# One transfer for each head: the bias table of a neighbourhood attention, stored as each query and head needs it

## The chip, the cores and the metric

The kernel runs on one core of one Trainium2 chip. The metric is the time of one execution on the device in microseconds (us); the median of three runs of the kernel before is 2916.8 us (2911.22 to 2920.01). The core has TensorE (PE, with its weight loads shown as PEld), VectorE (DVE), ScalarE (ACT), GpSimd (POOL) and SyncE (SP). SP computes nothing: it issues the transfers, and 16 DMA engines carry them out.

## The reference, cut to what matters

An encoder layer with two attention branches. The one that matters here is the neighbourhood attention: 8 heads of 64 channels over a grid 64 columns wide (2048 tokens of a sample and 512 of a prompt, so 32 and 8 rows). A query sees a window of 8 rows and 16 columns, and to each score a learned bias is added that depends on head, row distance and column distance alone:

```python
drow = key_rows - r[:, None]
dcol = jnp.clip(kc - qcol[:, :, None], -(NA_COLS - 1), NA_COLS - 1)
bias = rel_bias[h_idx, r_idx, c_idx].astype(jnp.float32)
s = jnp.einsum('brnqhd,brknchd->brnqhkc', qb, kb).astype(jnp.float32) / math.sqrt(dh) + bias
s = jnp.where(col_ok[:, :, None, None, :], s, NEG)
```

The other branch is a dilated band attention in three groups. Both are weighted by gates, projected, merged and projected again.

## The kernel before, in words

**Stages.** `run` goes through the dilated branch (`dil_sweeps`), the neighbourhood branch (`na_sweeps`), the gates and branch projections (`gate_sweeps`) and the last projection (`out_sweep`). `na_sweeps` works in two halves of four heads. In each half it goes over 20 tiles of 128 tokens (16 of the sample, 4 of the prompt): `bank` multiplies a tile by the q and k weights (512 columns) and by the v weights (256 columns), and `na_qk` and `na_v` normalise the result, split it into two fp16 parts and turn it by transposing transfers (`qn<-qs`, `kT<-qs`) or store it (`vd<-v`). Once six tiles are there, `na_group` starts the attention of 8 grid rows: 4 column blocks of 128 queries (8 rows by 16 columns), each in units of one head or two.

**Where the bias enters.** `load_bias` (L977) fills a table `G`, 128 queries by 4 heads by 16 by 48 values of float32. Partition `16 i + c` belongs to the query in row `i` and column `c` of a block, and holds a 16 by 48 cut of the padded, reversed bias of each head. ACT scales the four heads of `G` in place (`scale`, L991). `bias` in `na_group` (L1148) then lets POOL add a mask to a window of `G` and write `bm`, which DVE adds to the scores (`e<-s,bm`). There is one `G`; the second half's table goes to the same place, and its load is started when the 60 additions of the first half are planned (`na_bias`, L933).

In memory the table is `bias`, 8 row shifts by 8 heads by 16 by 63 values. `load` (L983) is called four times, `BIAS_STEP` = 4 us of planned time apart, and issues two transfers each time. Each fills 16 partitions with 64 pieces of 48 values (192 bytes), so a half takes 8 transfers with 1024 pieces each. The four scalings are planned after the fourth call, 4 us apart.

**What sets the order.** Each engine carries out its instructions in the order in which they were emitted, and nothing is put in another order at run time. That order comes from a planner (`Clock`, L109): every step is put on a heap with a due time, and each instruction adds a planned cost to its engine's time. A transfer (`dma`, L388) costs SP 0.48 us and the DMA engines its bytes at 340,000 a us (`D_RATE`), without regard to the size of its pieces, and counts as landed 1.2 us after that. Other steps hang on gates: the additions on `bias_ready` (L932, four signals, one from each scaling), a unit's scores on its additions (`go`, L1232).

**What runs beside it.** Right after the first half's table is called for, `na_weights(1)` (L961) loads the weights of the second half in two banks: each `load_bank` (L422) issues `wr<-in_w_in` transfers of 256 KB in pieces of 1 KB or 2 KB, DVE takes maxima of them (`wm`), PE turns the maxima (`across`, L474, a transpose at L356) and spreads them, and ACT and DVE make the fp16 weights `wt`. Beside the second half's table, `gate_weights(0)` does the same for the gates. All of these, the transposing transfers and the table are issued by SP, one after the other, on one queue.

Of the kernel before, what the change touches and what calls it, by code (L numbers as in the profile page):

```python
# [104 lines left out]
BIAS_STEP = 4.0  # L105
# [159 lines left out]
class Enc:  # L265
# [711 lines left out]
    def load_bias(self, half):  # L977


        G = self.G = self.N["g"].tile([128, 4, 16, 48], F32, name="G")  # L980
        t = self.a["bias"]

        def load(qr):  # L983
            for i in range(qr, qr + 2):
                self.dma(G[16 * i:16 * i + 16],
                         AP(t.tensor, (8 * i + 4 * half) * 16 * 63, [[1, 16], [63, 64], [1, 48]]))
            if qr == 6:
                for h in range(4):
                    self.clk.at(self.clk.done + BIAS_STEP * h, scale, h)

        def scale(h):  # L991
            self.act(G[:, h], G[:, h], scale=self.sc[0][:, 2:3])
            self.bias_ready[half].signal()

        for i in range(4):
            self.clk.at(self.clk.now + BIAS_STEP * i, load, 2 * i)

    def na_v(self, R, seq, i, ps):
        half = seq["half"]
# [1078 lines left out]
def masks():  # L2078
    m = np.zeros((128, C_W), np.float32)
    q = np.arange(128)[:, None]  # L2080
    j = np.arange(256)[None]
    band = np.where((j >= q) & (j <= q + 128), 0, NEG)
    m[:, C_BAND:C_BAND + 256] = band
    m[:, C_BAND + 256:C_BAND + 384] = band[:, 0:128]
    j = np.arange(128)[None]
    m[:, C_B1:C_B1 + 128] = np.where(np.abs(j - q) <= 64, 0, NEG)
    m[:, C_BD:C_BD + 128] = np.where(j // 32 == q // 32, 0, NEG)
    cols, _ = window_masks()
    m[:, C_COL:C_COL + 96] = np.concatenate(cols, axis=1)
    return m  # L2090
# [15 lines left out]
def na_masks():  # L2106
    cols, rows = window_masks()
    m = [np.minimum(r[:, k0:k0 + n, None], c[:, None]).reshape(128, -1)
         for r, k0, n in zip(rows, (4, 0, 0), ROWS) for c in cols]
    return np.concatenate(m, axis=1).astype(ml_dtypes.bfloat16)  # L2110
# [9 lines left out]
def rope_table():  # L2120
    inv = np.array(INV_BITS, np.uint32).view(np.float32)
    ang = (np.arange(LS, dtype=np.float32)[:, None] * inv[None]).astype(np.float64)
    c, s = np.cos(ang), np.sin(ang)
    return np.ascontiguousarray(np.concatenate([c, c, -s, s], axis=1).astype(np.float32))


def arrays_of(inputs):
    b = np.zeros((8, 23, 63), np.float32)
    b[:, 4:19, 16:47] = np.asarray(inputs["rel_bias_a"])[0][:, ::-1, ::-1]

    b = np.stack([b[:, r:r + 16] for r in range(8)])
    a = {
        "x_prompt": np.asarray(inputs["x_prompt"])[0],
        "x_sample": np.asarray(inputs["x_sample"])[0],
        "norm_gain": inputs["norm_gain"],
        "w_in": np.asarray(inputs["w_in"])[0],
        "qn_a": inputs["qn_a"],
        "kn_a": inputs["kn_a"],
        "qn_b": inputs["qn_b"],
        "kn_b": inputs["kn_b"],  # L2140
        "w_a": np.asarray(inputs["w_branch_a"])[0],
        "w_b": np.asarray(inputs["w_branch_b"])[0],
        "w_out": np.asarray(inputs["w_out"])[0],
        "bias": b,
        "ident": np.eye(128, dtype=np.float32),
        "cmask": masks(),
        "namask": na_masks(),
        "cs": rope_table(),
    }
    return {k: np.ascontiguousarray(v) for k, v in a.items()}  # L2150
# [24 lines left out]
```

## Time and profile before

| | |
|---|---|
| median of the runs | 2916.8 us |
| the profiled execution's own time | 2913.82 us |
| its span, first to last instruction | 2912.0 us |
| PE busy | 2687.4 us (92%) |
| DVE, ACT, POOL busy | 1627.4, 1303.5, 1269.4 us |
| mean granted TensorE clock | 0.975 |
| DMA | 823504 packets, 419.20 MB, mean 144 GB/s |
| packets under 512 B | 706240 |
| `G<-in_bias` | 16 transfers of 192 KB |

Times in the trace are counted from the first instruction of the span. A busy share over the whole span mixes stages: the dilated branch lasts to about 1285 us, the neighbourhood branch to about 1850 us, and the gates and the last projection fill the rest. A line of waits names the engine that stood, and behind the arrow what ended its wait. SP's own rows carry a q (SPq), and their duration is the time it took to issue a transfer, not the time in which the data moved.

### The profile page before, as it was taken

Reading aid. Unit: us, or ns where it says so; the run is one execution under the profiler, and the core shown is the slowest. Engines: PE = TensorE matmul, PEld = TensorE weight load, DVE = VectorE, ACT = ScalarE, POOL = GpSimd, SP = SyncE. Lnnn points to the kernel's source line nnn. Section 1 sums busy time; section 2 is a strip of 40 time slices with the busy share of each in tenths; the row PEclk is TensorE's granted clock in tenths of the full one; section 3 lists DMA queues with packets and bytes.
Section 4 is the critical chain, followed back from the end, with each engine's and each line's share of the span. In section 5 each row is a group of like instructions: output and inputs, shape, how many; then the busy total and the mean of one; then the engine's idle time right before and its main releaser. Section 6 shows DMA issues by size and latency. Waiting matters only on the chain.

```text
span 2912.0 us, 55755 instructions
## 1 busy us (share of the span) xinstructions
PE 2687.4 (92%) x20841; PEld 1785.7 (61%) x20841; DVE 1627.4 (56%) x3902; ACT 1303.5 (45%) x3495; POOL 1269.4 (44%) x1787
## 2 busy tenths in 40 slices
PE   6898989989999999988888887799999999999999
PEld 2444444444444444444444445699999999999887
DVE  6887767785555754347786778531245544454111
ACT  6666666575655665545564556411123211222110
POOL 4777677667667887734553455100001100011110
PEclk9999999999999999999999998899999999999999
DMA  7899876775655655489989898431243444454443
GB/s 229 201 197 192 195 174 120 161 142 105 116 111 111 141 117 107 87 181 173 196 182 194 187 194 190 126 80 44 66 134 119 129 127 121 126 169 112 146 146 108
DMA packets 823504, 419.20 MB, mean 144 GB/s; under 512 B 706240, under 2 KB 750912, under 8 KB 816832
## 3 DMA queue, kind: packets, MB, share of 16 engines
q1 hardware_dynamic: 823232, 415.63, 62.5%
q8 instruction: 163, 2.67, 0.4%
q14 instruction: 109, 0.89, 0.1%
HBM read 171.72 MB, written 79.13 MB: 86 GB/s over the span
## 4 chain that ended last, share of the span: by engine, by line
PE 46%; DVE 15%; POOL 14%; ACT 9%; DMA 8%; issue 6%; SPq 2%; DVEq 0%; ACTq 0%; POOLq 0%
PE proj L352 36%; PE s L352 9%; POOL qk L377 7%; ACT e L360 5%; DVE e L365 4%; DMA pT<-p 4%; DVE p L365 3%; POOL sq L377 3%; POOL q_t L377 2%; DVE wm L365 1%; DVE q_ssq L365 1%; DMA qn<-qs 1%; ACT qs L360 1%; DVE qs L365 1%; DMA wr<-in_w_in 1%
## 5 line engine op out<-in xcount | busy, mean ns | idle before, releaser
L352 PEld LDWEIGHTS <-hb 128*128 128x128 f16 x6240 | 590.7, 99 | 615.9 <-issue 68.7
L352 PE MATMUL proj<-wt,hb 128*128 128x512 f16 (+2 forms) x3360 | 694.0, 359 | 5.8 <-DVE v L365 4.5
L352 PE MATMUL proj<-wu,hb 128*128 128x512 f16 x2880 | 665.6, 385 | 10.7 <-DVE wu L365 8.4
L360 ACT ACTIVATE e<-e,neg,sc 128x256 f32<-128x256 f32 (+4 forms) x688 | 392.9, 573 | 2.3
L360 ACT ACTIVATE sg<-proj,wi 128x256 f32<-128x256 f32 x240 | 113.2, 473 | 613.6 <-PE proj L352 605.9
L352 PEld LDWEIGHTS <-pT 128*128 128x128 f16 (+1 forms) x4560 | 222.6, 101 | 186.8 <-DMA pT<-p 127.3
L352 PE MATMUL proj<-hb,wt 128*128 128x256 f16 x2760 | 314.1, 273 | 7.8 <-DMA hb<-htd 7.4
L352 PEld LDWEIGHTS <-wt 128*128 128x128 f16 x2760 | 269.1, 98 | 41.1 <-issue 9.4
L365 DVE TENSOR_TENSOR p<-e,p 128x512 f16<-128x512 f32 (+2 forms) x302 | 265.6, 883 | 27.1 <-ACT p L360 22.3
L377 POOL TENSOR_TENSOR sq<-qk,gcs 128x256 f32<-128x256 f32 x240 | 181.9, 779 | 225.1 <-DVE q_ssq L365 210.2
L365 DVE TENSOR_TENSOR qk<-s,sg 128x256 f32<-128x256 f32 x160 | 67.9, 424 | 340.3 <-PE s L352 337.3
L352 PE MATMUL s<-hb,wt 128*128 128x256 f32 x1880 | 247.0, 285 | 0.0
L365 DVE CAST p<-e 128x512 f16<-128x512 f32 (+2 forms) x237 | 151.2, 639 | 168.8 <-ACT e L360 151.5
L352 PEld LDWEIGHTS s<-hb,wt 128*128 128x128 f32 x1880 | 231.0, 189 | 1.2 <-DVE wt L365 0.2
L352 PE MATMUL proj<-hb,kT 128*128 128x256 f16 x1920 | 225.9, 274 | 0.8 <-ACT sg L360 0.6
L360 ACT ACTIVATE qs<-qk 128x512 f16<-128x512 f32 (+1 forms) x200 | 106.8, 537 | 208.3 <-POOL qk L377 188.5
L352 PEld LDWEIGHTS <-kT 128*128 128x128 f16 x1920 | 183.7, 98 | 25.5 <-issue 1.1
L365 DVE TENSOR_TENSOR qs<-qk,qs 128x512 f16<-128x512 f32 (+1 forms) x169 | 122.8, 730 | 135.6 <-ACT qs L360 133.8
L377 POOL TENSOR_TENSOR hb<-sg,hb 128x256 fp32r<-128x256 f32 x19 | 18.9, 997 | 378.8 <-ACT hb L360 378.8
L377 POOL TENSOR_TENSOR qk<-qk,sq 128x512 f32<-128x512 f32 (+1 forms) x122 | 167.2, 1371 | 34.5 <-DVE qk L365 25.1
L365 DVE CUSTOM_DVE_ANT_0 e<-s,cmask 128x256 f32<-128x256 f32 (+2 forms) x528 | 151.6, 344 | 46.2 <-PE s L352 26.0
L377 POOL TENSOR_TENSOR qk<-qk,gcs 128x512 f32<-128x512 f32 x120 | 162.0, 1350 | 9.4
(182 smaller groups left out, 3724.8 us busy)
## 6 DMA issues: line engine op xcount, KB each, us to landing
hb<-htd SPq DMA_DIRECT2D x40, 1024.0 KB
wr<-in_w_in SPq DMA_DIRECT2D x132, 256.0 KB
obd<-osb SPq DMA_DIRECT2D x50, 264.0 KB
hd<-xs SPq DMA_DIRECT2D x20, 512.0 KB
htd<-hb SPq DMA_DIRECT2D x10, 1024.0 KB
mad<-qk SPq DMA_DIRECT2D x40, 256.0 KB
e<-obd SPq DMA_DIRECT2D x40, 256.0 KB
sq<-mad SPq DMA_DIRECT2D x40, 256.0 KB
```

What stands on the lines that cost most here:

```text
L352: self.nc.tensor.matmul(out, a, b, start=start, stop=stop, **kw)
L360: self.nc.scalar.activation(out, x, func, **kw)
L365: getattr(self.nc.vector, ins)(out, *a, **kw)
L377: getattr(self.nc.gpsimd, ins)(out, *a, **kw)
```

## The change

The host lays the table out by half, query, head and the 16 by 48 cut, so that one query and head is one piece of 3072 bytes. One transfer fills one head of `G`, 128 partitions at once. The four transfers of a half are called for 4 us of planned time apart, as the four calls were, and each scaling is planned for when its own transfer is planned to have landed.

```diff
@@ load_bias
-        def load(qr):
-            for i in range(qr, qr + 2):
-                self.dma(G[16 * i:16 * i + 16],
-                         AP(t.tensor, (8 * i + 4 * half) * 16 * 63, [[1, 16], [63, 64], [1, 48]]))
-            if qr == 6:
-                for h in range(4):
-                    self.clk.at(self.clk.done + BIAS_STEP * h, scale, h)
+        def load(h):
+            self.dma(G[:, h], t[half, :, h])
+            self.clk.then(scale, h)
...
-        for i in range(4):
-            self.clk.at(self.clk.now + BIAS_STEP * i, load, 2 * i)
+        for h in range(4):
+            self.clk.at(self.clk.now + BIAS_STEP * h, load, h)
@@ arrays_of
-    b = np.stack([b[:, r:r + 16] for r in range(8)])
+    b = np.stack([b[:, r:r + 16, c:c + 48] for r in range(8) for c in range(16)])
+    b = b.reshape(128, 2, 4, 16, 48).transpose(1, 0, 2, 3, 4)
```

`arrays_of` runs on the host ahead of the launch and is not part of the time.

## Rows read from the trace of the kernel before

**Rows 1.** The page, busy time of engines, and slices of 72.8 us
```profile
PE 2687.4 (92%) x20841; PEld 1785.7 (61%) x20841; DVE 1627.4 (56%) x3902; ACT 1303.5 (45%) x3495; POOL 1269.4 (44%) x1787
...
PE   6898989989999999988888887799999999999999
...
DMA  7899876775655655489989898431243444454443
```

**Rows 2.** Windows by stage: length, busy of five engines, clock, DMA share, GB/s
```profile
1285.00:1340.00 55.00, 44.19 (x248) 25.25 (x246) 30.04 (x69) 19.45 (x43) 14.87 (x37) 0.88 1.09 186
1562.00:1617.00 55.00, 40.25 (x265) 22.94 (x263) 24.54 (x60) 18.39 (x47) 17.09 (x39) 0.88 1.20 195
1340.00:1560.00 220.00, 190.84 (x1737) 108.36 (x1736) 184.64 (x443) 130.20 (x367) 115.80 (x169) 0.98 0.91 192
1617.00:1850.00 233.00, 187.54 (x1792) 113.86 (x1791) 183.16 (x463) 141.93 (x380) 119.72 (x160) 0.91 0.87 185
1850.00:2912.00 1062.00, 1056.73 (x8397) 947.10 (x8397) 380.12 (x801) 202.16 (x427) 81.69 (x70) 1.00 0.38 115
```

**Rows 3.** Waits in 1285 to 1340 us: total us, times, longest
```profile
PE proj L356 <- DVE wm L365: 10.5, 2, 5.4
```

**Rows 4.** Waits of PE in 1562 to 1617 us
```profile
PE o L352 <- DMA pT<-p: 9.2, 3, 5.7
PE proj L352 <- DVE v L365: 4.2, 1, 4.2
PE proj L352 <- DMA hb<-htd: 1.3, 1, 1.3
```

**Rows 5.** DMA in 1296.6 to 1298.6 us
```profile
DMA packets 866, 0.16 MB, mean 82 GB/s; under 512 B 866, under 2 KB 866, under 8 KB 866
```

**Rows 6.** DMA in 1303 to 1305 us
```profile
DMA packets 794, 0.76 MB, mean 382 GB/s; under 512 B 48, under 2 KB 794, under 8 KB 794
```

**Rows 7.** Timeline of SP, 1280 to 1360 us: start, length, what, count
```profile
1285.55 1.07 SPq L395 DMA_DIRECT2D G<-in_bias  x2
1286.73 4.14 SPq L400 DMA_TRANSPOSE qn<-qs  x1
...
1292.61 1.86 SPq L395 DMA_DIRECT2D G<-in_bias  x2
1294.53 7.30 SPq L395 DMA_DIRECT2D wr<-in_w_in  x8
...
1303.12 3.18 SPq L395 DMA_DIRECT2D G<-in_bias  x2
...
1311.26 3.35 SPq L395 DMA_DIRECT2D G<-in_bias  x2
```

**Rows 8.** Timeline, 1575 to 1640 us: rows of SP
```profile
1574.28 3.89 SPq L395 DMA_DIRECT2D vd<-v  x1
...
1578.27 2.34 SPq L400 DMA_TRANSPOSE pT<-p  x1
```

**Rows 9.** Chain of work in order of time: start, us, what
```profile
1294.53 7.30 DMA wr<-in_w_in
...
1306.40 15.53 DMA qn<-qs x2
...
1583.95 7.58 DMA pT<-p
```

**Rows 10.** The tile G: its transfers (ns min/median/max), and idle time they ended
```profile
L395 SPq DMA_DIRECT2D G<-in_bias x16: 321/574/2727, 1285.6 to 1593.5; - x16
...
  DMA G<-in_bias: 7.1, 1
```

**Rows 11.** Timeline, 1575 to 1640 us: an addition of POOL and ACT's last scaling
```profile
1610.90 3.90 POOL L377 TENSOR_TENSOR bm<-G,namask 128x384 f32<-128x384 f32 x4
...
1611.30 0.92 ACT L360 ACTIVATE G<-G,sc 128x768 f32<-128x768 f32 x1
```

**Rows 12.** Waits in 1340 to 1560 us
```profile
PE s L352 <- DVE mx L365: 21.1, 24, 3.1
```

## The prediction

> **What bounds the kernel now.** I read the page first, then windows by stage, then the waits inside the two stages in which the table is loaded, and last the queue that serves them. The page shows PE busy for 92% of the span, so time comes back only where PE stands or runs at the lower clock [rows 1]. The slices show where: from about 1240 to 1890 us PE is at 7 or 8 tenths, and the DMA engines are near full. The windows split that stretch [rows 2]. The first table is loaded in 1285 to 1340 us (stretch A), the second in 1562 to 1617 us (stretch B). PE is busy for 44.19 and 40.25 of 55 us there, so it stands 10.8 and 14.8 us, and the granted clock is 0.88 in both. After 1850 us PE is busy for 1056.73 of 1062 us: what A and B lose is not made up later.
>
> The waits name what PE stood for. In A two waits hold 10.5 us, both for the maxima `wm` of the weight loads [rows 3]. In B three waits for `pT` transfers hold 9.2 us, one for `v` 4.2 and one for `hb` 1.3 [rows 4]. All of them lead to the one queue, and the chain of work says the same: a `wr` load for 7.3 us, two `qn` transfers for 15.53 us, a `pT` transfer for 7.58 us [rows 9].
>
> In the queue the table is the slow traffic. In 1296.6 to 1298.6 us only packets under 512 B move, and 0.16 MB over 866 of them is the table's 192 bytes to rounding: 82 GB/s [rows 5]. In 1303 to 1305 us the `wr` loads in pieces of 1 KB run at 382 GB/s [rows 6]. A half of the table is 8 x 196,608 bytes, 1.573 MB, so at 82 GB/s it holds the DMA engines for 19.2 us, or 4.8 us for each pair of transfers.
>
> **The change, part by part. The transfers.** 8 per half become 4, and 16,384 pieces in all become 1024. For a piece of 3072 bytes the trace has no row. The ends are 82 GB/s (nothing gained) and 382 GB/s; I take 382, since its pieces of 1 KB are nearest and the new ones are larger still. A half then takes 4.1 us, 1.03 us a transfer, and the queue is free 15.1 us sooner in each stretch.
>
> [...]
>
> **SP.** The eight issues took 1.07 + 1.86 + 3.18 + 3.35 = 9.5 us in A [rows 7]. Four at the median of 0.574 us [rows 10] are 2.3, so SP is 7.2 us earlier behind them. Behind them stand the eight `wr` loads, `qn` and `kT`, and SP is held by the full queue in between (`qn` took 4.14 us to issue, `vd` in B 3.89) [rows 7, 8].
>
> **Stretch A.** The first wait (10.5 − 5.4 = 5.1 us) ends with `wr` loads that stand behind the first two pairs of the table. These two pairs shrink from 9.6 to 2.1 us, the loads come 7.5 us sooner, more than 5.1: the wait goes whole, −5.1. For the second (5.4) to go, the second bank must come 10.5 us sooner. The queue gives 15.1, and the two `qn` transfers, between whose issue and landing lie the third and fourth pair, should shrink by 7.5. But DVE's and ACT's work on the first bank is on that path too; between 0 and 5.4 I take half, −2.7.
>
> **Stretch B.** The queue is relieved by the same 15.1 us. The longest `pT` wait (5.7) is for a transfer issued at 1578.27 behind a `vd` that was held for 3.89 us, with table pieces ahead; this and the `hb` wait should go, the two shorter `pT` waits hardly: −5.7 − 0.3 − 1.3. The wait for `v` (4.2) comes through ACT, which stood 7.1 us for `G` [rows 10] with the next tile's work queued behind it. Each scaling still waits for a transfer, so I take half, −2.1. Together −9.4.
>
> [...]
>
> **The scalings.** Their number and their 0.92 us stay. They move some 12 us of planned time ahead on ACT, past a tile's squares, q and k parts, and each waits for its own transfer, where before the first of four waited for all. One such wait costs between 0 and the 7.1 us of the row [rows 10]. ACT is busy for only 19 of 55 us [rows 2], and covers most of it; if that cover is gone, DVE, SP's transposes and PE's accumulators wait behind ACT. I take +2 in all. No new order between transfers and scalings arises: POOL's addition at 1610.90 reads head 0 while ACT still scales head 3 at 1611.30 [rows 11], so heads are tracked apart, and load h + 1 need not wait for scaling h.
>
> **The order.** All four `bias_ready` signals come 12 planned us sooner, so in the second half the additions and first scores may be put up to 12 us earlier among the projections. By how much that helps is not in the trace: between −12 (all of it) and +12 (scores put ahead of projections that PE then does not reach). I take 0, since PE's waits in the units are short (24 for DVE, 21.1 us in all [rows 12]) and there are projections on either side.
>
> **Sum.** −5.1 − 2.7 − 9.4 − 2.5 − 2.5 + 2 = −20.2 us, against the profiled execution's 2913.8 (span 2912.0, 1.8 around it): 2893.6. The median of the runs is 3.0 above that execution, so I forecast 2897 for the median.
>
> **Rivals.** [...]
>
> Second, **no change**: what A and B give back is lost to other waits, to `qn` and `pT` transfers that come late anyhow or to the new order: 2909 to 2925, about 2915. For it: in 1340 to 1560 us DVE is busy for 184.64 of 220 us, so units that start sooner may only wait sooner. Against it: the sequence is fixed on each engine, and a shift ahead of a stage carries through. It also takes in that the change does not do what it says (2 in 100), and that a small piece costs little more than its bytes (3 in 100): then something else held the queue to 82 GB/s, the table's share of the relief is lost, and only SP's 7.2 us a half are left, which PE sees little of. [...]
>
> Third, **slower**: ACT stands. A scaling comes right behind its load in the plan, but the load can sit behind eight `wr` loads (7.3 us [rows 7]). If all eight scalings stand for 7.1 us, ACT loses 57 us in stretches in which it has 2 x 36 idle. It decides once ACT's standing goes beyond what four accumulators cover, about a tile. If four of the eight reach PE at 4.2, the size of the wait for `v` in B [rows 4], 17 us come on top; the waits of A and B then stay as long as they are, with ACT in the queue's place, but for the first of 5.1: +12, about 2929.
>
> **How the numbers follow.** Forecast 0.55 (−12 to −28), more 0.13, no change 0.21, slower 0.11. About 0.3%, 9 us, is what a measurement can tell from no change. Faster takes the first two, 0.68; same 0.21; slower 0.11. The range goes from 2879 (the most that the sum gives, less some) to 2921 (no change with its scatter); it leaves out the slow case and the far end of the second.
>
> **What would show it.** Right: packets under 512 B fall by 16,384 on the page; `G<-in_bias` appears 8 times at 384 KB; DMA in A shows no stretch of 82 GB/s with only small packets but for the transposes; the `wm` wait of 5.1 and the `pT` wait of 5.7 are gone, and PE stands under 8 us in each stretch. Wrong: ACT waits for `G` of over 15 us in total, PE waits for `v` in their place; or stretches A and B shorter, but the stretch from 1340 to 1560 or from 1617 to 1850 us longer by as much.

## The result, and the profile after

The changed kernel takes 2882.82 us (median of 4 runs, 2881.67 to 2884.74) against 2917.97 us for the kernel before, run beside it. The ratio is 0.9892, with a 95% interval of 0.9877 to 0.9906. The profiled execution took 2881.97 us with a span of 2880.2 us, 31.8 us less than the span before; between the medians it is some 35 us.

The page of the changed kernel: busy time of the engines, slices of 72.0 us, and the packets.

```profile
PE 2680.1 (93%) x20841; PEld 1782.3 (62%) x20841; DVE 1630.3 (57%) x3905; ACT 1300.8 (45%) x3493; POOL 1271.7 (44%) x1788
...
PE   6899998989989999999888987899999999999999
...
DMA  7888976766655655468999998332144444353443
...
DMA packets 808017, 419.20 MB, mean 146 GB/s; under 512 B 689729, under 2 KB 734401, under 8 KB 801345
```

The bytes are the same and so is PE's busy time to 0.3%; 16,511 small packets are gone. Over the neighbourhood branch (slices 18 to 26) PE's digits read 998889878 where they read 888888877 [rows 1]. The windows by stage, with the columns of [rows 2] (start:end and length; PE, PEld, DVE, ACT, POOL busy; clock, DMA share, GB/s), show where. First the two stretches in the kernel before, cut to the same 60 us as those of after:

```profile
1280.00:1340.00 60.00, 49.19 (x292) 28.71 (x290) 31.76 (x73) 21.26 (x48) 15.98 (x42) 0.89 1.08 191
...
1560.00:1620.00 60.00, 44.80 (x298) 25.27 (x295) 29.03 (x72) 19.86 (x52) 20.54 (x43) 0.89 1.19 191
```

And the changed kernel:

```profile
1280.00:1340.00 60.00, 59.44 (x396) 34.89 (x395) 43.78 (x107) 29.05 (x72) 24.53 (x51) 1.00 0.89 232
1340.00:1560.00 220.00, 191.07 (x1717) 106.89 (x1714) 184.44 (x432) 132.37 (x368) 119.11 (x180) 0.97 0.94 200
1560.00:1620.00 60.00, 52.36 (x409) 28.53 (x408) 39.26 (x101) 28.87 (x81) 27.78 (x49) 0.91 0.93 196
1620.00:1850.00 230.00, 190.91 (x1814) 127.89 (x1813) 180.12 (x437) 127.14 (x336) 102.58 (x132) 0.90 0.83 180
1850.00:2880.00 1030.00, 1025.28 (x8132) 918.45 (x8130) 364.48 (x769) 192.44 (x406) 79.91 (x69) 1.00 0.38 115
```

In stretch A PE stood 10.8 us of 60 and now stands 0.6, at the full clock, and it finishes 396 matmuls where it finished 292. The stretch in between is as it was [rows 2].

For stretch B these windows mislead, since the changed kernel is some 17 us ahead by then: it issues its second table from 1545.80 to 1565.03 us, where the kernel before issued it from 1562.50 to 1592.90. So B has to be compared over the same work. PE's order there is the same in both kernels, from the `o` matmuls just ahead of the table to the matmul that waits for `v`. These are rows of PE's timeline (start, length, what, and in brackets the idle time before and what ended it), first in the kernel before:

```profile
1561.79 0.52 PE L352 MATMUL o<-vc,pT 128*128 128x64 f16 x12 [0.46 <-DMA pT<-p]
...
1607.13 9.89 PE L352 MATMUL proj<-wt,hb 128*128 128x512 f16 x51 [4.23 <-DVE v L365]
```

and in the changed kernel:

```profile
1545.12 0.52 PE L352 MATMUL o<-vc,pT 128*128 128x64 f16 x12 [0.40 <-DMA pT<-p]
...
1578.89 2.72 PE L352 MATMUL proj<-wt,hb 128*128 128x512 f16 x6 [3.81 <-DVE v L365]
```

The windows between these two matmuls, the kernel before first:

```profile
1561.80:1607.10 45.30, 30.58 (x213) 17.86 (x214) 20.15 (x53) 13.53 (x36) 10.42 (x24) 0.88 1.27 189
...
1545.10:1578.90 33.80, 27.04 (x214) 16.30 (x215) 19.77 (x50) 15.51 (x38) 11.86 (x25) 0.98 1.06 255
```

The same matmuls take 11.5 us less. PE stands 6.8 us instead of 14.7, which is 8.0 less, and it is busy 3.5 us less, at a clock of 0.98 instead of 0.88.

PE's waits of the changed kernel, with the columns of [rows 3]; the first row is from 1280 to 1345 us, the other three from 1535 to 1625 us:

```profile
PE o L352 <- DMA pT<-p: 0.6, 1, 0.6
...
PE o L352 <- DMA pT<-p: 6.2, 8, 1.5
...
PE proj L352 <- DVE v L365: 3.8, 1, 3.8
...
PE s L352 <- DVE mx L365: 0.6, 2, 0.4
```

The two `wm` waits of 10.5 us are gone from A [rows 3]. In B the `pT` wait of 5.7 us and the `hb` wait are gone, and the wait for `v` is 3.8 us where it was 4.2 [rows 4]. Of the eight `pT` waits of these 90 us only five lie in the same work as above: 3.3 us in all, where the kernel before had four of 9.7 us.

The queue behind this, SP's timeline of the changed kernel (start, us to issue, what, count):

```profile
1282.45 0.43 SPq L395 DMA_DIRECT2D namask<-in_namask  x1
1282.92 0.46 SPq L395 DMA_DIRECT2D G<-in_bias  x1
1283.75 1.39 SPq L400 DMA_TRANSPOSE qn<-qs  x1
...
1286.58 0.61 SPq L395 DMA_DIRECT2D G<-in_bias  x1
1287.55 4.27 SPq L395 DMA_DIRECT2D wr<-in_w_in  x8
...
1293.83 0.33 SPq L395 DMA_DIRECT2D G<-in_bias  x1
...
1297.96 0.58 SPq L395 DMA_DIRECT2D G<-in_bias  x1
```

The last piece of the table is issued 15.0 us after the first; before it took 25.7 us (1311.26 − 1285.55) [rows 7]. SP is held for 1.39 us by the first `qn`, where it was 4.14, and for 4.27 us by the `wr` loads, where it was 7.30.

To say where the 32 us came from I followed instructions that both kernels have. `namask`, issued just ahead of the first table, stands at 1285.08 us before and at 1282.45 us after. Ahead of it the two programs are the same, so these 2.6 us are scatter between executions. The tile rows give the first and last start of an instruction: in the kernel before,

```profile
L377 POOL TENSOR_TENSOR bm<-G,namask x96: 904/1152/1606, 1332.5 to 1805.3; 128x384 f32<-128x384 f32 x48, 128x512 f32<-128x512 f32 x48
...
L395 SPq DMA_DIRECT2D oad<-oparts x40: 603/633/745, 1365.7 to 1852.8; - x40
```

and in the changed kernel:

```profile
L377 POOL TENSOR_TENSOR bm<-G,namask x96: 901/1150/1607, 1315.7 to 1763.3; 128x384 f32<-128x384 f32 x48, 128x512 f32<-128x512 f32 x48
...
L395 SPq DMA_DIRECT2D oad<-oparts x40: 598/632/1282, 1350.2 to 1819.9; - x40
```

The first output (`oad`) is 15.5 us sooner, the last 32.9 us, and the span ends 31.8 us sooner. Between the two outputs, PE's rows above show the start of B 16.7 us sooner and its end 28.2 us. So A gives 12.9 us beyond the scatter, the units of the first half 1.2, stretch B 11.6, the rest of the second half 4.7, and the last third takes 1.1 back. A split like this is good to some 2 us: inside the first half the lead moves, and one run of scores there starts 19.1 us sooner (1542.83 before, 1523.76 after).

### The profile page after: what moved, and what is told of

Same layout as the page of the kernel before. It is cut to its first block, busy times and chain, and to the rows that moved or that the text cites. A ratio compares the mean times of both kernels' runs of the same rounds, so it can differ in the third digit from the quotient of the medians.

```text
span 2880.2 us, 55778 instructions
## 1 busy us (share of the span) xinstructions
PE 2680.1 (93%) x20841; PEld 1782.3 (62%) x20841; DVE 1630.3 (57%) x3905; ACT 1300.8 (45%) x3493; POOL 1271.7 (44%) x1788
## 4 chain that ended last, share of the span: by engine, by line
PE 47%; DVE 16%; POOL 14%; ACT 8%; DMA 7%; issue 6%; SPq 2%; DVEq 0%; ACTq 0%; POOLq 0%
PE proj L352 37%; PE s L352 9%; POOL qk L377 7%; ACT e L360 4%; DVE p L365 4%; DVE e L365 4%; POOL sq L377 3%; DMA pT<-p 2%; POOL q_t L377 2%; DVE wm L365 1%; DVE q_ssq L365 1%; DMA qn<-qs 1%; DVE qs L365 1%; DVE wt L365 1%; SPq L395 1%
## 5 line engine op out<-in xcount | busy, mean ns | idle before, releaser
L352 PE MATMUL proj<-wt,hb 128*128 128x512 f16 (+2 forms) x3360 | 685.8, 356 | 3.8 <-DVE v L365 3.8
L377 POOL TENSOR_TENSOR hb<-sg,hb 128x256 fp32r<-128x256 f32 x18 | 17.7, 984 | 380.3 <-ACT hb L360 278.8
```

The costliest lines, as they stand in the source:

```text
L352: self.nc.tensor.matmul(out, a, b, start=start, stop=stop, **kw)
L377: getattr(self.nc.gpsimd, ins)(out, *a, **kw)
```

## Experiments

Each result is a median and a ratio with its 95% interval against the kernel before on the same chip; e1 to e4 share one chip (before: 2914.69 us), e5 to e8 one (2914.00 us), e9 to e12 one (2910.99 us).

**e1: the larger pieces alone.** The kernel before, in its order, with its eight transfers to 16 partitions each; but the table lies in memory so that a piece has 3072 bytes.

```diff
-    b = np.stack([b[:, r:r + 16] for r in range(8)])
+    b = np.stack([b[:, r:r + 16, c:c + 48] for r in range(8) for c in range(16)])
+    b = b.reshape(128, 2, 4, 768).transpose(1, 0, 2, 3)
+    b = np.pad(b, ((0, 0), (0, 0), (0, 0), (0, 32)))
...
-                self.dma(G[16 * i:16 * i + 16],
-                         AP(t.tensor, (8 * i + 4 * half) * 16 * 63, [[1, 16], [63, 64], [1, 48]]))
+                self.dma(G[16 * i:16 * i + 16].rearrange("p h r c -> p h (r c)"),
+                         t[half, 16 * i:16 * i + 16, :, 0:768])
```

> The eight transfers and the instruction order of the kernel before on every engine; only the memory layout differs, so that each partition's share comes in pieces of 3072 bytes. Theory P (the pieces of 192 bytes hold the queue, nothing else matters much): the wait for wm of 5.1 us and the pT wait of 5.7 us are gone, the time is 2884 to 2895, 23 to 34 us under the kernel before. Theory O (the gain comes from scalings and scores that are put earlier): within 6 us of the kernel before. Theory I (fewer issues on SP): within 8 us of the kernel before, since 16 transfers are still issued.

Measured: 2904.05 us (2895.95 to 2909.18), ratio 0.9964 [0.9950, 0.9979]. That is 0.36%, about a third of the change's 1.08%. Two windows of DMA in which nearly only the table moves, 1299 to 1300.9 and 1310.9 to 1312.6 us:

```profile
DMA packets 111, 0.29 MB, mean 154 GB/s; under 512 B 16, under 2 KB 16, under 8 KB 111
...
DMA packets 100, 0.25 MB, mean 149 GB/s; under 512 B 17, under 2 KB 18, under 8 KB 100
```

Pieces sixteen times as large bring 82 GB/s [rows 5] to about 150, not to the 382 that I took. Something else holds this transfer. The 10.6 us that came are in none of the three ranges expected, neither that of the pieces (23 to 34) nor those of the order (up to 6) or of SP's issues (up to 8).

**e2, e3: the changed kernel with small pieces again.** Its order and its four transfers to 128 partitions; the pieces are cut to 192 bytes (`n = 1`) and 384 bytes (`n = 2`) by 15 unused values behind each.

```diff
+    b = np.pad(b.reshape(2, 128, 4, 16 // n, 48 * n), ((0, 0),) * 4 + ((0, 15),))
...
-            self.dma(G[:, h], t[half, :, h])
+            self.dma(G[:, h].rearrange("p (a r) c -> p a (r c)", r=n),
+                     t[half, :, h, :, 0:48 * n])
```

> The instruction order and the eight transfers of the changed kernel, but the rows of the table are padded in memory, so that each transfer moves 2048 pieces of 192 bytes. Theory P: the gain is lost, 2908 to 2935, and above the kernel before if ACT, which now waits for each head on its own, stands for over 15 us in all. Theory O: 2880 to 2892. Theory I: 2885 to 2897.

> As the run with 192 bytes in the new order, but two rows lie together: 1024 pieces of 384 bytes in a transfer. If a small piece costs a fixed time (192 bytes at 82 GB/s are 2.3 ns a piece over the 16 engines), a half takes 9.6 us, and about two thirds of what 192 bytes lose comes back: 2890 to 2908. If what counts is that a piece is under 512 bytes, the rate stays near 82 GB/s and the time is that of the run with 192 bytes within 5 us.

Measured: 2895.33 us for 192 bytes, 0.9928 [0.9904, 0.9952], and 2886.22 us for 384 bytes, 0.9903 [0.9878, 0.9927]. With the small pieces of the kernel before, two thirds of the gain are there, so the range of the pieces (2908 to 2935) failed; 2895 lies in the one expected of fewer issues on SP, which e6 tests. The run with 384 bytes missed both of its ranges: it is 9.1 us under the run with 192 bytes, though their intervals overlap. DMA of the kernel with 192 bytes, 1293.1 to 1294 us:

```profile
DMA packets 1150, 0.22 MB, mean 244 GB/s; under 512 B 1150, under 2 KB 1150, under 8 KB 1150
```

Only small packets move, and at three times the rate of [rows 5]. The piece size alone is not what made 82 GB/s.

**e4: the scalings planned as before.** The changed kernel's transfers, but all four scalings are planned after the last transfer.

```diff
-            self.clk.then(scale, h)
+            if h == 3:
+                for j in range(4):
+                    self.clk.at(self.clk.done + BIAS_STEP * j, scale, j)
```

> The changed kernel's four transfers with large pieces, but the four scalings are planned as before, after the fourth transfer and 4 us apart. Theory P: 2880 to 2897, as fast as the changed kernel within some us, as scores wait for other things. Theory O: the gain is mostly lost, 2905 to 2920.

Measured: 2889.15 us (2881.28 to 2895.75), 0.9912 [0.9877, 0.9946]. The interval takes in the changed kernel's whole, so what the earlier scalings bring is not to be separated from nothing; no engine waits for `G`, and no wait for `wm` is left. The transfers carry most of the gain.

**e5, e6: only the partitions.** Two things differ between e1 and e2, the order and the number of partitions that a transfer fills. So in these two the kernel before keeps its order, its eight transfers of 192 KB and its calls; each transfer now fills half of one head's rows on all 128 partitions. In e6 the pieces stay at 192 bytes (`n = 1`), in e5 they have 1536 (`n = 8`). The host lays the table out to match, with 15 unused values behind each piece (not shown in the cut below).

```diff
-                self.dma(G[16 * i:16 * i + 16],
-                         AP(t.tensor, (8 * i + 4 * half) * 16 * 63, [[1, 16], [63, 64], [1, 48]]))
+                h, k = i // 2, i % 2
+                m = 8 // n
+                self.dma(G[:, h, 8 * k:8 * k + 8].rearrange("p (a r) c -> p a (r c)", r=n),
+                         t[half, :, h, m * k:m * k + m, 0:48 * n])
```

> The order of the kernel before on every engine and its eight transfers a half of 192 KB, but each transfer goes to all 128 partitions (half of a head's rows, pieces of 1536 bytes) instead of 16. Theory W (a transfer that goes to 16 partitions is the slow one, whatever its pieces): the transfers run at over 250 GB/s, the wm wait of 5.1 us is gone, 2884 to 2894, the gain of the change but for some us of the order. Theory O (the order carries what the large pieces alone did not): 2900 to 2910, as with large pieces to 16 partitions.

> As the run before it, with pieces of 192 bytes: the order and the piece size of the kernel before, and only the partitions of a transfer differ. Theory W: a pair of transfers holds the queue for some 1.7 us, as small pieces to 128 partitions did in the new order, not 4.8; 2890 to 2902. Theory P (pieces): 2908 to 2920, no change. Theory O: 2905 to 2920.

Measured: e6 2892.53 us (2886.27 to 2902.54), 0.9923 [0.9902, 0.9943]; e5 2889.29 us (2885.5 to 2893.28), 0.9912 [0.9895, 0.9928]. With the pieces, order and number of transfers of the kernel before, the partitions alone give 0.77% of 1.08%. Since eight transfers a half are issued as before, fewer issues on SP are not what brings it. DMA of e6 from 1285 to 1286 us, with the queue's share of 16 engines (from 1299.9 to 1301 us it is 262 GB/s):

```profile
DMA packets 1276, 0.24 MB, mean 241 GB/s; under 512 B 1276, under 2 KB 1276, under 8 KB 1276
...
q1 hardware_dynamic: 1276, 0.24, 123.3%
```

PE's waits of e6, the first two from A, the last from B:

```profile
PE proj L356 <- ACT qs L360: 3.3, 1, 3.3
...
PE proj L356 <- DVE wm L365: 0.9, 1, 0.9
...
PE o L352 <- DMA pT<-p: 5.5, 6, 2.7
```

The `wm` waits fall from 10.5 to 0.9 us, with 3.3 us for ACT's `qs` in their place, and the longest `pT` wait is 2.7 us instead of 5.7, with no change in the size of a piece. Between e6 and e5 the larger pieces give another 0.11%, less than the intervals can separate.

**e7: the changed kernel once more,** unaltered, beside these.

> The changed kernel, beside the others on one chip: 2880 to 2888.

Measured: 2885.73 us (2878.4 to 2889.25), 0.9896 [0.9878, 0.9914]. It lies 3 us above the first measurement, with the same ratio within the intervals.

**e8: calls 2 us apart.** The changed kernel with

```diff
-BIAS_STEP = 4.0
+BIAS_STEP = 2.0
```

> The changed kernel with the four transfers of a half planned 2 us apart instead of 4. The scalings and additions may come up to 6 us of planned time earlier. If the place of the scores in the order is worth time, 2874 to 2882; if not, 2878 to 2892, no different from the changed kernel by over 0.3%.

Measured: 2892.05 us (2887.5 to 2894.06), 0.9918 [0.9901, 0.9936]. Calling for the table sooner did not help; if anything it cost some 6 us. PE has a wait for `wm` in A again (1.6 us). SP's timeline shows three of the four table transfers ahead of the `wr` loads (1287.45 us and two from 1291.14, `wr` from 1292.48), where the changed kernel has two. That this costs the 6 us would fit, but was only argued.

**e9 to e11: a ladder of partitions.** The transfers of the kernel before read overlapping memory: one partition's window lies 4 bytes beside the next. In these three each partition has a source of its own, in pieces of 192 bytes as before (the host's part of the cut is first), and each of the eight transfers fills 16, 32 or 64 partitions (`P`; `k = P // 16`, `nh = 4 // k`). The order is that of the kernel before.

```diff
-    b = np.stack([b[:, r:r + 16] for r in range(8)])
+    b = np.stack([b[:, r:r + 16, c:c + 48] for r in range(8) for c in range(16)])
+    b = b.reshape(128, 2, 64, 48).transpose(1, 0, 2, 3)
+    b = np.pad(b, ((0, 0),) * 3 + ((0, 15),))
...
+                p, h = P * (i // k), nh * (i % k)
+                self.dma(G[p:p + P, h:h + nh].rearrange("p h r c -> p (h r) c"),
+                         t[half, p:p + P, 16 * h:16 * h + 16 * nh, 0:48])
```

> The order, the transfers to 16 partitions and the pieces of 192 bytes of the kernel before; only the source differs: each partition reads memory of its own, where before 16 partitions read stretches that overlap but for 4 bytes. Theory W (the 16 destination partitions make a transfer slow): 82 GB/s as before, 2908 to 2920. Theory S (16 engines that read nearly the same addresses make it slow): the transfers run at over 200 GB/s, 2886 to 2902.

> As the run with 16 partitions and memory of its own, but a transfer goes to 32 partitions and two heads. Theory W: between 82 GB/s and the 235 GB/s of small pieces to 128 partitions, near 160; 2895 to 2906. Theory S: as with 16 partitions.

> As the run with 32 partitions, but 64 partitions and one head. [...]

Measured: e9 2914.44 us, 1.0007 [0.9998, 1.0017]; e10 2895.41 us, 0.9947 [0.9932, 0.9962]; e11 2901.13 us, 0.9959 [0.9946, 0.9972]. DMA of e9 (16 partitions) from 1297 to 1298 us:

```profile
DMA packets 450, 0.09 MB, mean 86 GB/s; under 512 B 450, under 2 KB 450, under 8 KB 450
...
q1 hardware_dynamic: 450, 0.09, 150.4%
```

e10 (32 partitions) from 1295 to 1296 us:

```profile
DMA packets 995, 0.19 MB, mean 191 GB/s; under 512 B 992, under 2 KB 995, under 8 KB 995
```

e11 (64 partitions) from 1288 to 1289 us:

```profile
DMA packets 1137, 0.22 MB, mean 215 GB/s; under 512 B 1137, under 2 KB 1137, under 8 KB 1137
```

e9 is the kernel before to 0.07%, at its rate and with its `wm` waits (10.3 us, the longest 5.4): the overlapping source costs nothing that could be measured. Each step of the ladder beyond 16 partitions has the same pieces, bytes, number of transfers and calls; what differs is the partitions that a transfer fills, and with them the stretches of memory that it reads. 32 partitions bring half of the change's gain. 64 are not better in time (0.9959 against 0.9947); e11 is above 200 GB/s in the window shown. e6 with 128 goes further than either (0.9923).

The windows shown are single microseconds, and in e10 and e11 the rate moves: e10 is at 164 GB/s from 1294 to 1295 us, and e11 from 1305 to 1306 us, again with little but the table's packets, is

```profile
DMA packets 822, 0.16 MB, mean 157 GB/s; under 512 B 822, under 2 KB 822, under 8 KB 822
```

A longer view is the time in which packets of the table are under way, summed over all transfers of a half from the packet records of the trace (gaps under 0.1 us are counted in, and other traffic may move beside them). It stands in the table below. By it 16 partitions take 17.7 and 19.6 us, 32 take 11.4 and 12.3, 64 take 10.8 and 13.0, and 128 take 9.6 and 10.2.

The number of partitions alone does not give e1, where pieces of 3072 bytes to 16 partitions reached 149 to 154 GB/s, against 82 to 86 for pieces of 192 bytes to 16. What in the chip makes the rate rise with the partitions was not shown.

**e12: the scaling 2 us later.** The changed kernel, each scaling planned 2 us behind its transfer's planned landing.

```diff
-            self.clk.then(scale, h)
+            self.clk.at(self.clk.done + 2.0, scale, h)
```

> The changed kernel with each scaling planned 2 us later than its transfer's planned landing. ACT's waits for the table (6.4 us in five waits in the changed kernel) shrink to under 3 us. If these waits reach PE, 2876 to 2882; if not, 2880 to 2892, as the changed kernel.

Measured: 2881.44 us (2877.16 to 2883.44), 0.9897 [0.9882, 0.9912]. What waited for `G`, by the tile's view, in the changed kernel:

```profile
ACT G L360: 6.4, 5
```

and in e12:

```profile
ACT G L360: 1.3, 2
```

ACT's waits shrink from five to two, by 5.1 us, and the ratio is that of e7 (0.9896): these waits cost nothing that could be measured. The time alone does not decide it, since 2881 lies in both of the ranges expected. No version that was run is separated from the changed kernel on the fast side.

The runs by what their table transfers do: the rate in windows of the table alone, and the time under way of half a table, in A and in B. In the kernel before that time is 16.7 and 19.4 us.

| run | partitions, piece | GB/s in windows | under way in A and B, us | ratio |
|---|---|---|---|---|
| e9 | 16, 192 B | 86 | 17.7, 19.6 | 1.0007 |
| e1 | 16, 3072 B | 149 to 154 | 12.8, 14.8 | 0.9964 |
| e11 | 64, 192 B | 157 to 215 | 10.8, 13.0 | 0.9959 |
| e10 | 32, 192 B | 164 to 191 | 11.4, 12.3 | 0.9947 |
| e6 | 128, 192 B | 241 to 262 | 9.6, 10.2 | 0.9923 |
| e5 | 128, 1536 B | no such window | 6.7, 6.4 | 0.9912 |
| changed (e7) | 128, 3072 B | no such window | 5.9, 7.6 | 0.9896 |

The ratio follows the time under way. Where two runs are alike in it (e10 and e11, e5 and e7) their intervals overlap as well; neighbours further apart in it overlap too, so the order of the whole table says more than any one step.

## Why the prediction was right, and where its reason was wrong

**The forecast.** 2897 us from 2879 to 2921; it was 2883. The sign and the case (faster) were right; the size, −31.8 us between the spans instead of −20.2, lies beyond the −12 to −28 of the forecast, in the case "more" (0.13). That the time lies in the stated range, near its lower end, is in part luck: the sum took the whole relief for the larger pieces, and the step below shows that they alone bring a third.

**The path from queue to PE: right.** The relief of the one queue takes PE's waits away (it stands 0.6 us instead of 10.8 in A, 6.8 instead of 14.7 over B's work), and a shift ahead of a stage carries through to the end (the lead of 16.7 us at the start of B is 28.2 at its end and 31.8 at the end of the span). The runs with the order of before show it: the less time the table is under way, the shorter the kernel (e9, e1, e10 and e11, e6, e5: from 17.7 and 19.6 us at a ratio of 1.0007 to 6.7 and 6.4 us at 0.9912). "No change" fell for that reason, as the prediction argued.

**The price of the small piece: the step that failed.** The prediction read 82 GB/s [rows 5] as what a piece of 192 bytes costs, and compared it with 382 GB/s for pieces of 1 KB [rows 6]. These two rows differ in a second thing, which I didn't look at: the table's transfers fill 16 partitions each. e6 moves the same pieces to 128 partitions at 241 to 262 GB/s, and e1 moves pieces of 3072 bytes to 16 partitions at about 150. Of the two factors the partitions weigh more: alone they give 0.77% [0.57, 0.98], the pieces alone 0.36% [0.21, 0.50], both in the order of before 0.88% (e5, with pieces of 1536 bytes). The relief itself was put at 15.1 us a half; by the time under way it is some 11 (from 16.7 to 5.9 in A and from 19.4 to 7.6 in B, the changed kernel as e7). The change does both, so the relief came about for a reason that the prediction didn't name. A change that had only enlarged the pieces would have been forecast at nearly the same −20.2 us, and e1 brought some 10.

The chance of 3 in 100 for "a small piece costs little more than its bytes" was far too low: its condition, that something else held the queue to 82 GB/s, is what e6 shows with 241 to 262 GB/s for the same pieces. What the prediction inferred from it, that only SP's 7.2 us would be left, was wrong as well, since the change also widened the transfers.

**The terms of the sum.** SP: four issues take 0.46 + 0.61 + 0.33 + 0.58 = 1.98 us, 2.3 were forecast. For stretch A PE's rows of the two transposes of `wm` tell more than the mean clock. In the kernel before:

```profile
1308.55 0.37 PE L356 MATMUL proj<-ident,wm 128*1 128x128 f32 x1 [5.09 <-DVE wm L365]
...
1334.97 0.37 PE L356 MATMUL proj<-ident,wm 128*1 128x128 f32 x1 [5.42 <-DVE wm L365]
```

and in the changed kernel, where neither waits:

```profile
1301.02 0.27 PE L356 MATMUL proj<-ident,wm 128*1 128x128 f32 x1
...
1319.43 0.27 PE L356 MATMUL proj<-ident,wm 128*1 128x128 f32 x1
```

The second comes 15.5 us sooner, 12.9 beyond the scatter; −10.3 with the clock was forecast. Of the 12.9, 10.8 are waits (these two, and 0.3 for `v` between them), so some 2.1 are left for the clock, where 2.5 was taken. What was mis-sized is the second wait, which went whole and not by half: 2.7 us more. The first half's units gave 1.2 us where I had none.

Stretch B, over the same work: the `pT` waits fell by 6.4 us (6.0 forecast), `hb` went (1.3), and the wait for `v` fell by 0.4 instead of 2.1. PE's busy time fell by 3.5 us with the clock (2.5 forecast). Together that is the 11.5 us found, where −9.4 − 2.5 = −11.9 was forecast: B's sum was right, with the share of `v` too large and that of the clock too small. Beyond the forecast, then, the −31.8 us hold the second `wm` wait, the +2 for the scalings that did not appear, 1.2 us in the first half's units and 4.7 behind B in the second half, where the order was set to 0; 2.6 us are scatter, and 1.1 was lost again at the end. What gave the 4.7 us is open. e4 and e12 move the scalings, e8 moves the calls, and each result lies within some 6 us of the changed kernel's; the order isn't shown to be the cause.

No run shows the two terms of −2.5 us for the clock by themselves; what the traces show in their place are stretches with a granted clock of 0.50, in the kernel before among them these two, each beginning near the end of one of the two `wm` waits (columns as in [rows 2]):

```profile
1307.50:1312.50 5.00, 3.95 (x18) 2.74 (x19) 3.13 (x11) 2.11 (x6) 1.79 (x6) 0.50 1.35 170
1335.00:1340.00 5.00, 5.00 (x18) 2.00 (x19) 3.52 (x12) 1.46 (x5) 3.86 (x9) 0.50 0.44 87
```

In the changed kernel, without these waits, the clock is 1.00 over the whole of A.

**ACT.** +2 us was taken for the scalings' own waits; ACT waits 6.4 us in five places for `G`, where it was 7.1 in one [rows 10], and e12 shows that this costs nothing to be measured. The rival "slower" needed 57 us of it. Nor does PE's wait for `v` hang mainly on it, as the prediction had it: ahead of that wait ACT stands 3.78 us for `G` and a little later 3.32 us for a `vd` transfer.

```profile
1569.76 0.94 ACT L360 ACTIVATE G<-G,sc 128x768 f32<-128x768 f32 x1 [3.78 <-DMA G<-in_bias]
...
1575.83 0.38 ACT L360 ACTIVATE v<-proj 128x256 f16<-128x256 f32 x1 [3.32 <-DMA vd<-v]
```

These are rows of ACT's timeline in the changed kernel (columns as in PE's rows above). In e12 ACT stands only 1.3 us for `G` in B, in two places, yet its longest wait for a `vd` transfer is still 3.1 us and PE still waits 2.3 us for `v`: the `vd` transfer holds most of it.

**The signs given.** The small packets fell by 16,511 where 16,384 were counted. The transfers are 8 of 384 KB. PE stands 0.6 us in A and 6.8 in B, under 8 in each. The waits of 5.1 and 5.7 us are gone, and the stretches behind A and B did not grow: the lead rises in both.

**Open.** How what is beyond e6's 0.77% is divided among larger pieces, fewer transfers and order: the versions lie within some 6 us of each other, which is about what their intervals can tell apart. Why 3072 bytes to 16 partitions reach 150 GB/s where 192 bytes reach 86 wasn't tried further. Nor was it separated whether the partitions themselves are what counts, or the stretches of memory read, which are wider apart when a transfer fills more partitions.

## What to carry to other kernels

When a transfer runs far below what its queue moves at other times (here 82 against 382 GB/s), read two things beside its row, the size of a piece and the number of partitions that it fills, and compare it with a transfer that differs in only one of them. Cutting a load so that each transfer fills all partitions can be worth more than making its pieces longer (here 0.77% against 0.36%), and it needs no other layout of the bytes within a piece. On the queue that several stages share here, the hold of one transfer is paid by others: its price stands in the waits for `wm` (10.5 us), `pT` (9.2) and `hb` (1.3), and in no wait of PE for the table.

## What the runs showed that was not expected

A window in which the packets take over 150% of the 16 engines' time and yet move only 82 to 86 GB/s (150.4% in e9, and 152.1% in the kernel before in the window of [rows 5], below) shows DMA engines that are full of a transfer that hardly moves: the same pieces to 128 partitions take 123% of it and move 241 GB/s (e6).

```profile
q1 hardware_dynamic: 866, 0.16, 152.1%
```

Whether such a transfer is held where it is read or where it is written was not shown. 64 partitions are no better than 32 in time (0.9959 [0.9946, 0.9972] against 0.9947 [0.9932, 0.9962]). And sources that overlap by all but 4 bytes from one partition to the next cost nothing measurable (e9, 1.0007 [0.9998, 1.0017]).
